# TensorE's order from the out-projection on: chosen by the scheduler, or as written

## Chip, cores, metric

The kernel runs on one core of a Trainium2 chip. The metric is the device time of one execution in microseconds (us), the median over several runs.

## What is computed

One decoder layer in float32 on 2048 tokens of width 1024. Attention and a gating unit share one input projection; their outputs, side by side, go through the out-projection, a residual and a layer norm, and then through a gated feed-forward net with 22 blocks of 128 hidden columns on either side (gate and up), again with residual and layer norm:

```python
mix = jnp.concatenate([attn, sgu], axis=-1) @ w_out[l] + b_out[l]
h = layer_norm(ALPHA * h + mix, ln_mix_g[l], ln_mix_b[l])
ffn = (jax.nn.silu(h @ w_gate[l]) * (h @ w_up[l])) @ w_down[l]
h = layer_norm(ALPHA * h + ffn, ln_ffn_g[l], ln_ffn_b[l])
```

The change touches these three matrix products (out, gate/up, down) and nothing ahead of them.

## The kernel before

**Units of seven products.** Each of the three matrix products is cut into units. A unit takes a 2 by 2 block of left tiles times a 2 by 2 block of right tiles with seven block products instead of eight (a Strassen-Winograd form). There are 76 units in a fixed order: 8 "o" (out-projection), 44 "g" (gate/up: half 0 of the tokens with 22 units, then half 1 with 22), 24 "d" (down-projection: three groups d0, d1, d2 of 8). A product is 4 matmul triples (3 in d0) of 512 columns; a triple is high times high, high times low, low times high part, since every float32 operand is split into a high and a low part.

**Order in a unit.** `CHAIN` is `a11→X, s1→Z, s2→X, s4→Z, s3→X, a12→Y, a22→X`: product → PSUM bank. X takes four products and Z two, one on top of the other. After each product a hook reads the bank, and the next product into that bank waits for that hook: s2 waits for the hook of a11, s4 for that of s1, s3 for that of s2, a22 for that of s3. In gate/up the hooks of a11, s1 and s2 are copies on ScalarE (L1114); those of s4, s3 and a12 are additions on VectorE (L1117), and that of s3 (`z<-X_g`) is the one that a22 waits for. The hook of a22 is L1132, and its result is stored by GpSimd (L1134). In "o" and "d" units all hooks are VectorE additions (L1030, L1032). "d2" also has a layer norm on VectorE (L133 to L167) and the stores of the output (L1178).

**Operands.** `Left.make(p)` makes the left operand of product p of the *next* unit right behind product p of this one: a sum on VectorE where needed (L888, L891, L894, L897), the high part on ScalarE (L864), the low part on VectorE (L865). Seven buffers hold a unit's left operands. `Right.make(p)` does the same for the right side (L929 on ScalarE, L930 on VectorE, differences L935 on VectorE), which changes only between stages: o to g half 0, half 0 to half 1, g to d0, d0 to d1, d1 to d2. There is one buffer for each of the seven right operands, so the new one is made after the last unit of the old side has used the old one. The right sides of g half 0 and of the d groups come ready-made (`pre`); that of half 1 also needs the L935 differences.

**Side work.** `combine` (L980 to L984) makes the d right sides in half 1, units 1 to 11, from loads L1152. `z_transpose` (L1074 on TensorE, 16 groups of 8) stands in units 1 to 8. `z_affine` runs in units 3 to 18 of half 0: a load of `za` on the SyncE queue (L1084), a multiplication and an addition on GpSimd over 128x1024 (L158, L159), and a store (L1086).

**What sets the order.** A scheduler with a timeline of its own orders each engine's instructions; every engine then takes its queue strictly in order and waits on semaphores. Before the change TensorE's queue is ordered in this way too. The line that issues all matmuls is L994, and the loop over the units stands at the end of `hybrid_block`.

Of the kernel before, what the change touches and what calls it, by code (L numbers as in the profile page):

```python
# [68 lines left out]
def hybrid_block(ctx, tc, x, pos, ln_col, ln_in_g, ln_in_b, wqkv, wsu, wsv, b_qkv, b_su, b_sv, sinks,  # L69
# [5 lines left out]
    def pool(stack, name, bufs, **kw):  # L75
        return stack.enter_context(tc.tile_pool(name=name, bufs=bufs, reuse_waits="tile", **kw))
# [43 lines left out]
    def bcast(row_ap, name, p=None, tag="cst"):  # L120
        t = (p or cst).tile([P, D], F32, tag=tag, name=name, **({"bufs": 1} if tag == "rq" else {}))
        SP.dma_start(t, row_ap.partition_broadcast(P))
        return t
# [851 lines left out]
    def combine(nm, load, k):  # L975

        t = raw8(f"tc_{nm}_{k}").rearrange("p (q t) -> p q t", q=4)
        for n, q in enumerate(("b11", "b12", "b22", "b21")):
            load(q, t[:, n:n + 1], slice(k, k + 1))
        V.tensor_tensor(t[:, 0], t[:, 1], t[:, 0], ALU.subtract)  # L980
        V.tensor_tensor(t[:, 1], t[:, 2], t[:, 1], ALU.subtract)
        V.tensor_tensor(t[:, 2], t[:, 2], t[:, 0], ALU.subtract)
        V.tensor_tensor(t[:, 3], t[:, 3], t[:, 2], ALU.subtract)
        PL.dma_start(tD[nm][:, :, k, :], t)  # L984

    def unit(name, nk, left, right, hooks, after=None):
        bank = {}
        for n, (p, x_, first) in enumerate(CHAIN):
            if first:
                bank[x_] = psf.tile([P, 512], F32, tag="f", name=f"{x_}_{name}")  # L990
            lt, rt = left.t[p], right.t[BOF[p]]
            for k in range(nk):
                for m, (a, b) in enumerate(((0, 0), (0, 1), (1, 0))):
                    PE.matmul(bank[x_], lt[:, a, k, :], rt[:, b, k, :],  # L994
                              start=(first and k == 0 and m == 0),
                              stop=(k == nk - 1 and m == 2), skip_group_check=True)
            hooks[p](bank[x_])
            if after:
                after(p)


    def load_m(j):
        t = raw8(f"rm{j}").rearrange("p (e a c) -> p e a c", e=2, a=2)
        for e in range(2):
            for a in range(2):
                SP.dma_start(t[:, e, a], mixd[2 * j + e][a].rearrange("p k t -> p (k t)"))
        v = t.rearrange("p e a (k t) -> p e a k t", k=4)
        return Left(f"o{j}", (v[:, 0, 0], v[:, 0, 1], v[:, 1, 0], v[:, 1, 1]), 4)
# [44 lines left out]
    def o_hooks(j):  # L1053
        ac = hacc.pop(j)

        def done(e):
            i = 2 * j + e
            mu, rs = moments(ac[e])
            nmr = small.tile([P, 1], F32, tag="nmr", name=f"nmr{i}")
            V.tensor_scalar(nmr, mu, rs, -1.0, ALU.mult, ALU.mult)  # L1060
            A.activation(ac[e], ac[e], AF.Identity, bias=nmr, scale=rs)
            PL.dma_start(zd[i], ac[e])
            zs[i] = ac[e]

        return block_hooks(ac, True, done)

    def z_transpose(i):
        z = zs.pop(i)
        for j in range(2):
            ps = psf.tile([P, 512], F32, tag="f", name=f"ph{i}_{j}")  # L1070
            tr = trp.tile([P, 4, P], F32, tag="tr", name=f"tr{i}_{j}")
            for k in range(4):
                kk = 4 * j + k
                PE.transpose(ps[:, k * P:(k + 1) * P], z[:, kk * P:(kk + 1) * P], ident)  # L1074
            for k in range(4):
                kk = 4 * j + k
                A.activation(tr[:, k], ps[:, k * P:(k + 1) * P], AF.Identity,
                             bias=mcol[:, 1, kk:kk + 1], scale=mcol[:, 0, kk:kk + 1])
            PL.dma_start(h2T[i // 4][:, 4 * j:4 * j + 4, (i % 4) * P:(i % 4 + 1) * P], tr)


    def z_affine(i):
        t = ot.tile([P, D], F32, tag="o", name=f"za{i}")
        SP.dma_start(t, zd[i])  # L1084
        affine(t, t, fg[0], fg[1])
        PL.dma_start(h2d[i], t)  # L1086
# [9 lines left out]
    def h_load(h):  # L1096
        def load(q, t, ks=slice(0, 4)):
            c, kk = {"b11": (0, 0), "b12": (1, 0), "b21": (0, 1), "b22": (1, 1)}[q]
            SP.dma_start(t, h2T[2 * h + c][:, 4 * kk + ks.start:4 * kk + ks.stop, :])
        return load  # L1100
# [45 lines left out]
    def d_load(g):  # L1146
        f0, n = GROUPS[g]
        nk = n // 2

        def load(q, t, ks=slice(0, nk)):  # L1150
            kk, c = {"b11": (0, 0), "b12": (0, 1), "b21": (1, 0), "b22": (1, 1)}[q]
            SP.dma_start(t, w_down[f0 + kk * nk + ks.start:f0 + kk * nk + ks.stop, :,  # L1152
                                   c * 512:(c + 1) * 512].rearrange("f p c -> p f c"))
        return load
# [31 lines left out]
    def load_left(u):  # L1186
        return {"o": lambda _, j: load_m(j), "g": load_w, "d": load_a}[u[0]](*u[1:])

    def load_right(u):
        return {"o": lambda _: o_right(), "g": h_right, "d": d_right}[u[0]](u[1])  # L1190

    def load_out(u):
        if u[0] == "o":
            load_h(u[2])
        elif u[0] == "d":
            load_acc(*u[1:])
# [6 lines left out]
    for n, pc in enumerate(pieces):  # L1203
        forms["g", 1, 1 + n] = [pc]

    lefts[0] = load_left(units[0])
    rights[0] = load_right(units[0])
    load_out(units[0])
# [4 lines left out]
    for n, u in enumerate(units):  # L1213
        last = n + 1 == len(units)
        new = not last and units[n + 1][:2] != u[:2]
        if new:
            rights[n + 1] = load_right(units[n + 1])
            rights[n + 1].fetch()
        elif not last:
            rights[n + 1] = rights[n]  # L1220

        def after(p):
            if not last:
                lefts[n + 1].make(p)
            if new:
                rights[n + 1].make(p)
            if u in forms and p in ("s2", "a12"):
                for nm, k in forms[u][p == "a12":][:1]:
                    combine(nm, h_load(0) if nm == "h0" else d_load(int(nm[1])), k)
            if 0 < n <= NT // 2 and p in ("s4", "a12"):  # L1230
                z_transpose(2 * (n - 1) + (p == "a12"))

        if u == ("g", 0, 1):
            oo.close()
            fb_ = pool(ctx, "fb_", 2)
            fg = [bcast(mix_g, "mg", fb_, "f"), bcast(mix_b, "mb", fb_, "f")]
        if u == ("d", 1, 0):
            fg = [bcast(ffn_g, "fg", fb_, "f"), bcast(ffn_b, "fb", fb_, "f")]
        if u[0] == "g" and u[1] == 0 and 3 <= u[2] < 3 + NT:
            z_affine(u[2] - 3)  # L1240
        if not last:
            load_out(units[n + 1])
        hooks = {"o": lambda _, j: o_hooks(j), "g": gu_hooks, "d": d_hooks}[u[0]](*u[1:])
        nk = GROUPS[u[1]][1] // 2 if u[0] == "d" else 4
        unit("_".join(str(x_) for x_ in u), nk, lefts.pop(n), rights.pop(n), hooks, after)
        if n + 2 < len(units):
            lefts[n + 2] = load_left(units[n + 2])


# [56 lines left out]
```

## Time and profile before

| | |
|---|---|
| median of 3 runs | 1995.65 us (1995.31, 1995.65, 2001.1) |
| the profiled execution | 1998.47 us, span on the core 1996.4 us, mean granted TensorE clock 0.984 |
| TensorE matmuls busy | 1917.0 us, 96% of the span, 9126 instructions |
| VectorE busy | 1456.3 us, 73% |
| ScalarE busy | 843.2 us, 42% |
| GpSimd busy | 437.5 us, 22% |

The share of a whole span hides the stages, so the rows below go by stage and then to single waits. In a timeline row, what stands in brackets is how long the engine was idle just before the row and whose instruction ended that; a row with "x12" is 12 instructions in a run. PE is TensorE's matmul, PEld its weight load, DVE VectorE, ACT ScalarE, POOL GpSimd, SPq the queue of SyncE, which issues loads.

### The profile page before, as it was taken

The numbers are of one execution on the slowest core, as the hardware profiler recorded it, in microseconds if no ns is written. First come the engines' busy times: TensorE is split into PE (matmuls) and PEld (weight loads), VectorE is DVE, ScalarE is ACT, GpSimd is POOL, SyncE is SP. The second block draws the span as 40 slices with busy tenths as digits, with TensorE's granted clock in tenths as the row PEclk, the third lists the DMA queues.
The fourth block names the chain that finished last, engine by engine and source line by source line (L and its number), as shares of the span: only waits on it lengthen the run. The fifth ranks groups of instructions, "written<-read, shape, count | busy, mean of one in ns | idle before, by whom it ended". The sixth has DMA issues, their size and how long they took to land.

```text
span 1996.4 us, 24982 instructions
## 1 busy us (share of the span) xinstructions
PE 1917.0 (96%) x9126; PEld 1581.7 (79%) x9126; DVE 1456.3 (73%) x2335; ACT 843.2 (42%) x1637; POOL 437.5 (22%) x431
## 2 busy tenths in 40 slices
PE   5699999999999999999999999999999999999997
PEld 4587878799787888888888887888888787887876
DVE  6769998676877876766765976655556869668997
ACT  4466667632364763333333533333334324224220
POOL 1246766311032223332320000000000000000212
PEclk8799999999999999999999999999999999999999
DMA  9044443796667963333342475631223668557532
GB/s 317 13 136 140 143 148 117 158 302 237 231 212 235 342 239 148 116 148 124 141 158 75 158 253 187 214 148 65 94 72 126 229 232 305 181 176 257 176 108 105
DMA packets 154810, 347.56 MB, mean 174 GB/s; under 512 B 11328, under 2 KB 74816, under 8 KB 151104
## 3 DMA queue, kind: packets, MB, share of 16 engines
q1 hardware_dynamic: 119488, 231.67, 34.3%
q0 software_dynamic: 35200, 114.31, 15.9%
q8 instruction: 71, 1.16, 0.2%
q14 instruction: 51, 0.42, 0.1%
HBM read 219.06 MB, written 126.88 MB: 173 GB/s over the span
## 4 chain that ended last, share of the span: by engine, by line
PE 77%; DVE 9%; DMA 6%; issue 3%; ACT 3%; POOL 2%; SPq 0%; POOLq 0%; DVEq 0%; ACTq 0%
PE X_g L994 22%; PE Z_g L994 11%; PE X_d L994 10%; PE Y_g L994 6%; PE Z_d L994 5%; PE pu L601 5%; PE X_o L994 4%; PE Y_d L994 3%; PE pq L330 2%; PE psv L562 2%; PE Z_o L994 2%; DMA tc_d<-in_w_down 1%; PE pkv L330 1%; PE Y_o L994 1%; DVE st L133 1%
## 5 line engine op out<-in xcount | busy, mean ns | idle before, releaser
L864 ACT ACTIVATE ws<-s 128x512 fp32r<-128x512 f32 x176 | 109.8, 626 | 202.2 <-DVE s L897 106.4
L865 DVE TENSOR_TENSOR ws<-s,ws 128x512 fp32r<-128x512 f32 x176 | 134.8, 768 | 60.4 <-ACT ws L864 59.8
L864 ACT ACTIVATE wa<-rw 128x512 fp32r<-128x512 f32 x132 | 82.1, 627 | 194.7 <-PE X_g L994 168.9
L1134 POOL DMA_DIRECT2D aD<-x x44 | 23.7, 540 | 599.5 <-DVE x L1132 586.9
L994 PE MATMUL Y_g<-b21t_h,wa 128*128 128x512 f32 x528 | 140.7, 396 | 0.1
L994 PE MATMUL Z_g<-t1t_h,ws 128*128 128x512 f32 x528 | 136.5, 395 | 0.0
L994 PE MATMUL X_g<-b11t_h,wa 128*128 128x512 f32 x528 | 131.8, 397 | 0.0
L994 PE MATMUL X_g<-t4t_h,wa 128*128 128x512 f32 x528 | 130.5, 395 | 0.8 <-DVE z L1117 0.7
L994 PE MATMUL X_g<-t2t_h,ws 128*128 128x512 f32 x528 | 130.6, 395 | 0.0
L864 ACT ACTIVATE ws_d<-s_d 128x512 fp32r<-128x512 f32 (+1 forms) x96 | 56.0, 594 | 175.1 <-PE X_d L994 70.2
L994 PE MATMUL Z_g<-b22t_h,ws 128*128 128x512 f32 x528 | 128.8, 392 | 0.0
L994 PE MATMUL X_g<-t3t_h,ws 128*128 128x512 f32 x528 | 127.3, 390 | 0.0
L994 PEld LDWEIGHTS X_g<-t4t_h,wa 128*128 128x128 f32 x528 | 98.9, 188 | 25.5 <-DVE z L1117 1.6
L994 PEld LDWEIGHTS Y_g<-b21t_h,wa 128*128 128x128 f32 x528 | 99.1, 188 | 24.3 <-ACT wa L864 0.5
L994 PEld LDWEIGHTS Z_g<-t1t_h,ws 128*128 128x128 f32 x528 | 99.1, 188 | 24.1
L994 PEld LDWEIGHTS X_g<-t2t_h,ws 128*128 128x128 f32 x528 | 99.1, 188 | 24.1
L994 PEld LDWEIGHTS X_g<-b11t_h,wa 128*128 128x128 f32 x528 | 99.1, 188 | 23.8
L994 PEld LDWEIGHTS Z_g<-b22t_h,ws 128*128 128x128 f32 x528 | 99.1, 188 | 22.9
L1132 DVE TENSOR_TENSOR x<-X_g,x 128x512 f32<-128x512 f32 x44 | 30.3, 689 | 118.5 <-PE X_g L994 118.4
L994 PEld LDWEIGHTS X_g<-t3t_h,ws 128*128 128x128 f32 x528 | 99.1, 188 | 21.0
L330 PE MATMUL pq<-wq,hT 128*128 128x512 f32 x384 | 96.7, 402 | 1.3 <-DVE at L486 1.2
L865 DVE TENSOR_TENSOR wa<-rw,wa 128x512 fp32r<-128x512 f32 x132 | 90.4, 687 | 10.3 <-ACT wa L864 9.5
(283 smaller groups left out, 4337.2 us busy)
## 6 DMA issues: line engine op xcount, KB each, us to landing
rw<-in_w_gate SPq DMA_DIRECT2D x44, 512.0 KB, 3.9
rw<-in_w_up SPq DMA_DIRECT2D x44, 512.0 KB, 4.8
aD<-x POOLq DMA_DIRECT2D x44, 512.0 KB, 3.0
hTd<-hT SPq DMA_DIRECT2D x16, 1024.0 KB, 7.2
hTg<-hTd POOLq DMA_DIRECT2D x8, 2048.0 KB, 9.5
accd<-da POOLq DMA_DIRECT2D x32, 512.0 KB, 3.8
ra<-aD SPq DMA_DIRECT2D x16, 1024.0 KB, 8.4
da<-accd SPq DMA_DIRECT2D x32, 512.0 KB, 3.5
```

The source lines that it names most:

```text
L133: V.bn_stats(st[:, j, :], src[:, j * 512:(j + 1) * 512])
L330: PE.matmul(ps[:, :c1_ - c0], t[:, a, k, :], wq[k][:, b, c0:c1_], start=(k == 0 and n == 0), stop=(k == KT - 1 and n == 2))
L562: PE.matmul(pv_, t[:, a, k, :], wsv_t[k][:, b, :], start=(k == 0 and n == 0), stop=(k == KT - 1 and n == 2))
L601: PE.matmul(pu[:, j, :], wsu_t[k][:, a, hs], t[:, b, k, :], start=(k == 0 and n == 0), stop=(k == KT - 1 and n == 2))
L864: A.activation(hi, src, AF.Copy)
L865: V.tensor_tensor(lo, src, f32b(hi), ALU.subtract)
L994: PE.matmul(bank[x_], lt[:, a, k, :], rt[:, b, k, :], start=(first and k == 0 and m == 0), stop=(k == nk - 1 and m == 2), skip_group_check ...
L1132: V.tensor_tensor(v["x1"], ps, v["x1"], ALU.mult)
L1134: PL.dma_start(aD[g][h][:, e, :], v["o"].rearrange("p a t -> p (a t)"))
```

## The change

Around the loop over the units a manual schedule is switched on for TensorE alone. TensorE's instructions from the first out-projection matmul to the last keep the order in which the code writes them: one product after the other, one unit after the other. The orders of the other engines are still chosen by the scheduler, now around that given TensorE order.

```diff
@@ end of hybrid_block @@
+    written = ExitStack()
+    written.enter_context(tc.manual_schedule(engines={mybir.EngineType.PE}))
     lefts[0] = load_left(units[0])
...
         if n + 2 < len(units):
             lefts[n + 2] = load_left(units[n + 2])
+    written.close()
```

In the names below, `X_g_0_10` is bank X of gate/up half 0, unit 10; `wa22_0_10` is its left operand for a22, `ws1` that of s1; `t4t_h0` is the right operand of a22, `b21t` that of a12, `b11t` that of a11. First TensorE in half 0, where unit 9 goes over into unit 10, before:

```order
L994 MATMUL X_g_0_10_8581<-b11t_h0_6958,wa11_0_10_8460 128x512 x12
L994 MATMUL Z_g_0_10_8599<-t1t_h0_6984,ws1_0_10_8480 128x512 x11
L994 MATMUL X_g_0_9_8445<-t4t_h0_7171,wa22_0_9_8434 128x512 x12
L994 MATMUL Z_g_0_10_8599<-t1t_h0_6984,ws1_0_10_8480 128x512
L994 MATMUL Y_g_0_10_8674<-b21t_h0_7115,wa12_0_10_8553 128x512
L994 MATMUL X_g_0_10_8581<-t2t_h0_7009,ws2_0_10_8498 128x512 x12
L994 MATMUL Y_g_0_10_8674<-b21t_h0_7115,wa12_0_10_8553 128x512 x11
L994 MATMUL Z_g_0_10_8599<-b22t_h0_7033,ws4_0_10_8516 128x512 x12
L994 MATMUL X_g_0_10_8581<-t3t_h0_7080,ws3_0_10_8535 128x512 x12
```

and after:

```order
L994 MATMUL X_g_0_9_8447<-t3t_h0_7082,ws3_0_9_8401 128x512 x12
L994 MATMUL Y_g_0_9_8540<-b21t_h0_7117,wa12_0_9_8419 128x512 x12
L994 MATMUL X_g_0_9_8447<-t4t_h0_7173,wa22_0_9_8436 128x512 x12
L994 MATMUL X_g_0_10_8583<-b11t_h0_6960,wa11_0_10_8462 128x512 x12
L994 MATMUL Z_g_0_10_8601<-t1t_h0_6986,ws1_0_10_8482 128x512 x12
L994 MATMUL X_g_0_10_8583<-t2t_h0_7011,ws2_0_10_8500 128x512 x12
L994 MATMUL Z_g_0_10_8601<-b22t_h0_7035,ws4_0_10_8518 128x512 x12
L994 MATMUL X_g_0_10_8583<-t3t_h0_7082,ws3_0_10_8537 128x512 x12
```

Between s3 of a unit (`t3t`) and its a22 (`t4t`) stood a11 and s1 of the next unit, 23 matmuls; now a12 of the same unit stands there, 12 matmuls, and no product is cut in pieces.

Next VectorE in the same unit after the change, from the last hook of unit 9 to the hook that a22 of unit 10 waits for:

```order
L1132 TENSOR_TENSOR x1_0_9_8460<-X_g_0_9_8447,x1_0_9_8460 128x512
L865 TENSOR_TENSOR wa22_0_10_8572<-rw0_10_8439,wa22_0_10_8572 128x512
L865 TENSOR_TENSOR wa11_0_11_8598<-rw0_11_8575,wa11_0_11_8598 128x512
L865 TENSOR_TENSOR ws1_0_11_8618<-s1_0_11_8616,ws1_0_11_8618 128x512
L888 TENSOR_TENSOR s1_0_12_8752<-rw0_12_8711 128x512
L865 TENSOR_TENSOR ws2_0_11_8636<-s2_0_11_8634,ws2_0_11_8636 128x512
L897 TENSOR_TENSOR s2_0_11_8634<-rw0_11_8575,s2_0_11_8634 128x512
L1117 TENSOR_TENSOR x1_0_10_8596<-Z_g_0_10_8601,x1_0_10_8596 128x512
L865 TENSOR_TENSOR ws4_0_11_8654<-s2_0_11_8634,ws4_0_11_8654 128x512
L891 TENSOR_TENSOR s2_0_12_8770<-s1_0_12_8752,rw0_12_8711 128x512
L1117 TENSOR_TENSOR z1_0_10_8614<-X_g_0_10_8583,z1_0_10_8614 128x512
```

Before, the same stretch had the addition from bank Y ahead of that from bank Z, and the split `wa22` stood ahead of L1132, not behind it.

Last TensorE where half 0 ends (unit 21) and half 1 begins, before:

```order
L994 MATMUL X_g_1_0_10244<-b11t_h1_10086,wa11_1_0_10083 128x512
L994 MATMUL X_g_0_21_10068<-t3t_h0_7080,ws3_0_21_10021 128x512 x12
L994 MATMUL X_g_1_0_10244<-b11t_h1_10086,wa11_1_0_10083 128x512 x11
L994 MATMUL Z_g_1_0_10262<-t1t_h1_10113,ws1_1_0_10108 128x512 x12
L994 MATMUL X_g_0_21_10068<-t4t_h0_7171,wa22_0_21_10056 128x512 x12
```

and after:

```order
L994 MATMUL X_g_0_21_10070<-t3t_h0_7082,ws3_0_21_10023 128x512 x12
L994 MATMUL Y_g_0_21_10196<-b21t_h0_7117,wa12_0_21_10041 128x512 x12
L994 MATMUL X_g_0_21_10070<-t4t_h0_7173,wa22_0_21_10058 128x512 x12
L994 MATMUL X_g_1_0_10246<-b11t_h1_10088,wa11_1_0_10085 128x512 x12
L994 MATMUL Z_g_1_0_10264<-t1t_h1_10115,ws1_1_0_10110 128x512 x12
```

Here too the two products of the next unit that stood between s3 and a22 of unit 21 have moved behind its a22.

## Rows read from the trace of the kernel before

**Rows 1.** Busy us (instructions) of each engine by stage, TensorE clock, DMA.

```profile
core 0: us, PE busy (x) PEld busy (x) DVE busy (x) ACT busy (x) POOL busy (x), PEclk, DMA share, GB/s
512.00:686.00 174.00, 168.47 (x769) 136.42 (x770) 137.20 (x244) 97.90 (x188) 40.34 (x59) 0.98 0.72 251
686.00:1113.00 427.00, 427.00 (x1852) 345.71 (x1851) 296.53 (x375) 169.58 (x300) 113.66 (x80) 1.00 0.40 146
1113.00:1540.00 427.00, 426.08 (x1833) 343.71 (x1832) 273.35 (x415) 161.30 (x276) 19.77 (x33) 1.00 0.42 147
1540.00:1986.00 446.00, 441.94 (x1895) 354.73 (x1893) 357.40 (x560) 131.71 (x208) 48.51 (x62) 1.00 0.57 198
```

**Rows 2.** TensorE timeline: start, length, operation, [idle before it, released by].

```profile
366.43 5.49 PE L562 MATMUL psv<-wsv_b,h 128*128 128x512 f32 x12 [3.63 <-DVE hl L459]
...
519.39 3.04 PE L994 MATMUL X_o<-t2t_o,ws_o 128*128 128x512 f32 x12 [1.22 <-DVE hb L1030]
...
640.59 5.31 PE L994 MATMUL X_o<-t4t_o,wa_o 128*128 128x512 f32 x12 [4.21 <-DVE hb L1032]
...
1241.62 3.06 PE L994 MATMUL X_g<-t4t_h,wa 128*128 128x512 f32 x12 [0.72 <-DVE z L1117]
...
1678.76 0.50 PE L994 MATMUL Y_d<-b21t_d,wa_d 128*128 128x512 f32 x1 [0.90 <-ACT b21t_d L929]
...
1983.11 3.04 PE L994 MATMUL X_d<-t4t_d,wa_d 128*128 128x512 f32 x12 [1.15 <-DVE da L1032]
```

**Rows 3.** Windows around the wait at 640 us; columns as in the first group.

```profile
630.00:640.60 10.60, 6.39 (x33) 4.98 (x31) 10.60 (x23) 5.81 (x12) 3.46 (x5) 0.91 0.75 260
640.60:646.00 5.40, 5.40 (x15) 4.29 (x16) 2.08 (x6) 1.26 (x2) 1.70 (x3) 0.54 0.98 249
```

**Rows 4.** Timeline of all engines, one gate/up unit of half 0.

```profile
941.55 2.98 PE L994 MATMUL X_g<-b11t_h,wa 128*128 128x512 f32 x12
...
943.18 0.68 DVE L1117 TENSOR_TENSOR z<-X_g,z 128x512 f32<-128x512 f32 x1
943.78 0.68 DVE L865 TENSOR_TENSOR wa<-rw,wa 128x512 fp32r<-128x512 f32 x1
...
945.27 0.69 DVE L865 TENSOR_TENSOR wa<-rw,wa 128x512 fp32r<-128x512 f32 x1 [0.21 <-ACT wa L864]
945.99 0.33 SPq L1091 DMA_DIRECT2D rw<-in_w_gate  x1
...
946.90 0.37 SPq L1084 DMA_DIRECT2D za<-zd  x1
946.92 2.96 PE L994 MATMUL X_g<-t4t_h,wa 128*128 128x512 f32 x12
...
949.72 0.40 PE L994 MATMUL Z_g<-t1t_h,ws 128*128 128x512 f32 x1
...
952.69 2.58 POOL L158 TENSOR_TENSOR za<-za,mg 128x1024 f32<-128x1024 f32 x1 [1.24 <-DMA za<-zd]
...
954.34 1.48 DVE L865 TENSOR_TENSOR ws<-s,ws 128x512 fp32r<-128x512 f32 x1 [1.33 <-ACT ws L864]
...
955.35 2.74 POOL L159 TENSOR_TENSOR za<-za,mb 128x1024 f32<-128x1024 f32 x1
...
955.85 2.78 DVE L897 TENSOR_TENSOR s<-rw,s 128x512 f32<-128x512 f32 x1
```

**Rows 5.** Timeline, VectorE and TensorE, where half 0 goes over into half 1.

```profile
1102.65 2.36 DVE L930 TENSOR_TENSOR b11t_h<-b_h,b11t_h 128x1024 fp32r<-128x1024 f32 x2 [0.74 <-ACT b11t_h L929]
1104.93 2.35 DVE L935 TENSOR_TENSOR b_h<-b_h,b_h 128x1024 f32<-128x1024 f32 x2
...
1120.49 0.68 DVE L1117 TENSOR_TENSOR z<-X_g,z 128x512 f32<-128x512 f32 x1
...
1122.62 2.96 PE L994 MATMUL X_g<-t4t_h,wa 128*128 128x512 f32 x12
```

**Rows 6.** VectorE's waits, 1130 to 1400 us: who, for whom: us, times, longest.

```profile
DVE tc_d L980 <- DMA tc_d<-in_w_down: 39.4, 8, 7.3
```

## The prediction

> **What bounds the kernel now.** I read the stages first. From the out-projection to the last matmul TensorE is busy 168.47 of 174, 427 of 427, 426.08 of 427 and 441.94 of 446 us [rows 1]: it stands still for 5.53 + 0 + 0.92 + 4.06 = 10.5 us in 1474, and nothing else bounds this part. Then I looked for where it stands still. The large waits are 1.22 us at 519, 4.21 at 640, 0.72 at 1241, 0.90 at 1678 and 1.15 at 1983 [rows 2]; the rest are pieces under 1 us. In all of gate/up, 44 of the 76 units, there is one. The reader is to see in [rows 2] that most waits end on VectorE or on a split of an operand: TensorE waits for hooks and operands, not for loads. One more price: behind the 4.21 us the 12 matmuls took 5.31 us, where 12 elsewhere start 2.80 us apart (946.92 to 949.72) [rows 2, 4], about 2.35 us more; the granted clock there was 0.54 [rows 3], near the lower of its two levels (1.2 of 2.4 GHz). So the most that any order can give back is 10.5 + 2.35 = 12.9 us.
>
> **What the change takes away.** Not one matmul goes; only their places move. In the order of before, a11 and s1 of the next unit lie between s3 and a22 of a unit, so that the hook of s3 has some 5.4 us (941.55, where s3 ends, to 946.92) [rows 4]. In the written order only a12 lies there: 2.80 us. Against that stands that a12 is always there. The wait of 4.21 us is an out-projection unit in which a22 follows directly on s3; this case disappears, with its 2.35 us. I first count the 12.9 us as given back in full, and then add every wait that the written order makes, those that come again among them.
>
> Durations for that: a VectorE instruction over 128x512 starts 0.60 us after the one before (943.18, 943.78) [rows 4], one over 128x1024 takes 2.28 / 2 = 1.14 (1102.65 to 1104.93) [rows 5]. A unit is 7 x 2.80 = 19.6 us, in d0, with 9 matmuls for 12, 14.7. I count from the start of a11 (t = 0), so s3 ends at 14.0 and a22 is due at 16.8, and I take VectorE's instructions in the order that it has after the change.
>
> **Gate/up, half 0, with GpSimd's affine (16 units).** Without side work the hook of s3 starts at 14.0 and ends at 14.7: 2.1 us early. But [rows 4] show what GpSimd does to VectorE. L158 runs from 952.69 to 955.27 and L159 from 955.35 to 958.09; the split L865 that starts at 954.34 takes 1.48 us for 0.69 and ends 0.55 after L158; L897 takes 2.78 and ends 0.54 after L159. A VectorE instruction that falls under L158 or L159 is held to its end. Where does that pair fall now? The load of za is issued behind the loads of the weights, and these wait for the split wa22 (945.27, then 945.99); L158 starts 952.69 - 946.90 = 5.8 us after the issue of za [rows 4]. After the change wa22 is made at t = 0.7 to 1.4, za is issued at 2.3, and L158 starts at 8.1; the store of the unit's result, issued at about 0.8, now goes ahead of these loads. Three transfers of 512 KB land in 952.69 - 945.99 = 6.7 us, so a fourth can add up to a third, 2.2; I take 8.1 to 9.6 as likely. With 8.1 the split of ws2 (due at 9.1) is held to 11.2 and L897 to 14.0, then four instructions, and the hook of s3 ends at 16.4: just in time. With 9.3 L897 is held to 12.4 and, if an addition from PSUM is held as well, the Z hook to 15.2; the hook of s3 ends at 17.0: 0.3 late. With 11 it is 18.1: 1.4 late. No row shows an L1117 under L158 or L159, so between 0 and 1.4 us a unit is open; I take 0.25, near the 8.1 to 9.6 that the rows give: 16 x 0.25 = **4.0 us** (0 to 22). Cover before: 5.4 us, so it was free.
>
> The Trainium skill, page "SBUF — State Buffer", section "Who interferes with whom", says that a VectorE instruction with two SBUF inputs contends with a GpSimd instruction that reads SBUF, and one with at most one SBUF input does not. L865 and L897 held, as above, agree with the first half; for the second no row here has the case. By it the term would be near 0 in place of 4.0, and the hook of s3 itself never held.
>
> **Half 0 to half 1.** The right side of half 1 is made while unit 21 runs. Up to the hook of s3 VectorE has, behind the first halves of b11t at t = 5.0: 5 splits L930 and 5 differences L935 of 1.14, and 4 instructions of 0.60: 5.0 + 11.4 + 2.4 = 18.8, end 19.5. Before, the same hook ran at 1120.49 and a22 started at 1122.62 without a wait [rows 5], covered by a11 and s1 of half 1. Now a22 is due at 16.8: 2.8 us late. Behind it stand three more L930 and one L935, three left splits and two hooks ahead of the second half of t2t, so s2 of the new unit waits about 2.0 us more, and its a22, behind b21t, t4t and two L935, about 1.7. Together **6.5 us** (3 to 11, with one drop of the clock).
>
> **The borders of the down-projection.** d0 to d1, by the same count: between the a11 hook of d0's last unit (t = 2.7) and its s3 hook VectorE has six L930, two left splits and four hooks; the s3 hook ends at 14.2 and a22 is due at 12.6: 1.65. Then eight more instructions, five of 1.14, lie ahead of the hook of a11 of d1 that s2 waits for: 2.8. Together 4.45, where before TensorE waited 0.90 at 1678 [rows 2]. d1 to d2 has the same instructions in units of 19.6 us rather than 14.7: 2.4. g to d0: 1.1. Together **7.9 us** (4 to 11).
>
> **The out-projection.** Its first unit waits for the X_o hook of a11 as before (1.22 at 519 [rows 2]); since s1 now runs unbroken and the hook does not come earlier, 1.9, and behind it 1.2 for the operands of a12 and a22, which are still being split. The first unit of gate/up waits 1.8 for t3t and b21t of its new right side. Together **4.9 us** (3 to 7). The other o units have 21.4 us with the transposes and no wait by count.
>
> **Half 1 with combine; d2; the end.** VectorE now waits up to 7.3 us for a load at L980 [rows 6], and its place in the queue moves: in units 6 to 10 L980 stands a few rows earlier, right behind the splits. Whoever is queued behind it (ws splits with a unit's time in hand, the Z hook, the s3 hook) is late by that wait; with the largest wait, 7.3 us from t = 2.5 on, and eleven instructions of 0.60 behind it the s3 hook ends at 17.1, 0.3 late; with the mean, 39.4 / 8 = 4.9 us, it ends at 14.7, in time: 0 (0 to 4). In d2 VectorE also carries the layer norms; over the whole stage it is busy 357.40 of 446 us [rows 1], so a hook can come late there too: 0 (0 to 4). The last hook of row block e1 now follows a12's layer norm at only 2.8 us: **0.5** (0 to 1).
>
> **The sum.** 4.0 + 6.5 + 7.9 + 4.9 + 0.5 = 23.8 us of waits made, less 12.9 taken away: **+11 us**. The profiled execution took 1998.47 us (span 1996.4, the rest outside it), 2.8 above the median of 1995.65; I put the difference on the median: 1995.65 + 11 = 2006.7, say **2007 us**.
>
> **Rivals.** *The waits are covered (faster).* VectorE's order is chosen anew around the written TensorE order, and if it and the loads bring the hooks at the four borders 2 to 3 us earlier than I count, the borders cost what they cost now. Then 12.9 - 4.9 (out-projection and first unit) = 8 us are gained: 1988. It decides at one point: the s3 hook of unit 21 must end by t = 16.8. Against it: 18.8 is a sum of VectorE work alone, without any wait. *About the same.* Half of the border waits and little of the affine: 23.8 - 7.2 - 3 = 13.6 against 12.9, near 1997. *PSUM additions are not held by GpSimd:* the affine term is 0, 2003. The Trainium skill's page "SBUF — State Buffer" says so (above). *Each unit of half 0 waits:* L158 at t = 11 or later, 1.4 x 16 = 22 for 4, and the three waits of 2 to 3 us at borders each drop the clock: behind a wait of 3.63 us 12 matmuls took 5.49 us [rows 2], no row shows what a wait of 2 to 3 us does. 2007 + 18 + 3 x 2.35 = 2032. That the change would not do what it says is excluded by the order of TensorE's instructions.
>
> **Chances.** Measurement can tell 0.3%, 6 us, from no change. My forecast (2004 to 2014) 0.42; PSUM additions not held, 2003: 0.15, a third of it inside 0.3%; each unit waits, 2018 and up: 0.16; about the same: 0.14; covered: 0.13. Slower by over 0.3%: 0.42 + 0.10 + 0.16 = 0.68, less 0.05 for the part of the forecast that lands under it: 0.63. Same: 0.24. Faster: 0.13. The range reaches down to the covered case at 1989 and up into the case where each unit waits, 2026; I leave out the ends of both.
>
> **What would show it.** Right: TensorE's waits in [rows 1] grow from 10.5 to some 24 us; the row at 640 is gone with its clock of 0.54; new waits before `X_g<-t4t_h` released by L1117, a short one in each of 16 units of half 0 and one of 2 to 3 us where half 1 begins; waits before `X_d<-t4t_d` and `X_d<-t2t_d` at the starts of d1 and d2. Wrong: no wait in half 0 (GpSimd's pair falls earlier, or PSUM additions pass), or gate/up with waits in half 1 as well, where I count none: then VectorE's loads of combine decide, and the slack of 2.1 us is not there.

## The result, and the profile after

The changed kernel takes 2023.56 us (median of 5 runs, 2020.46 to 2028.44); the kernel before, in 5 runs on the same chip, 1995.65 us. The ratio is 1.0137, 95% interval 1.0119 to 1.0156: slower by 27.9 us. The sign of the prediction holds, and the time lies inside its range; its size does not hold: it said 2007, 11 us slower, and the change cost two and a half times that. The profiled execution took 2024.12 us with a span of 2022.4, that is 26.0 over the span before.

The windows view of the kernel after, by the stages of [rows 1] (columns as there; with a fifth stretch, because the last matmul now ends at 2011.5):

```profile
512.00:686.00 174.00, 170.32 (x787) 138.03 (x788) 141.99 (x249) 100.40 (x191) 40.76 (x60) 1.00 0.74 254
686.00:1113.00 427.00, 413.67 (x1772) 329.73 (x1771) 290.71 (x358) 164.39 (x287) 110.05 (x78) 1.00 0.39 142
1113.00:1540.00 427.00, 421.30 (x1806) 339.63 (x1805) 275.72 (x408) 165.60 (x272) 19.77 (x33) 1.00 0.41 145
1540.00:1986.00 446.00, 438.72 (x1874) 352.00 (x1874) 359.36 (x550) 142.18 (x220) 42.35 (x58) 1.00 0.58 201
1986.00:2012.00 26.00, 25.53 (x110) 20.28 (x109) 18.66 (x30) 1.90 (x3) 4.82 (x5) 1.00 0.17 61
```

TensorE's idle time in the out-projection fell from 5.53 to 3.68 us. In gate/up it rose from 0 and 0.92 to 13.33 and 5.70, in the down-projection from 4.06 to 7.28: in these four stages 30.0 us for 10.5, where the prediction had some 24. Half 0 of gate/up, which had no wait at all, is now the worst stage. Who ends the waits, from the end of the first gate/up unit to the last matmul (waits view of the kernel after, TensorE; us in total, times, longest):

```profile
PE X_g L994 <- DVE z L1117: 17.0, 19, 2.7
PE X_d L994 <- DVE da L1032: 6.6, 7, 1.9
PE X_g L994 <- ACT x L1114: 0.9, 1, 0.9
...
```

Nearly all are hooks on VectorE; none is for a load or for an operand. 16 of the 19 in the first row are in the 16 units of half 0 that have GpSimd's affine. One of them in TensorE's timeline, from its a11 to the next:

```profile
748.36 2.96 PE L994 MATMUL X_g<-b11t_h,wa 128*128 128x512 f32 x12
...
762.24 2.98 PE L994 MATMUL Y_g<-b21t_h,wa 128*128 128x512 f32 x12
765.97 3.06 PE L994 MATMUL X_g<-t4t_h,wa 128*128 128x512 f32 x12 [0.76 <-DVE z L1117]
768.87 2.96 PE L994 MATMUL X_g<-b11t_h,wa 128*128 128x512 f32 x12
```

From a11 to a11 it is 768.87 - 748.36 = 20.51 us, where an unhindered unit takes 19.49. A wait costs more than its bracket: behind a running product the next one starts 2.80 us after it, but a12's modelled end, from which the bracket counts, is 2.98 after its start; and the first product after a wait holds up the next by 2.90 instead of 2.80. 0.76 + 0.18 + 0.10 = 1.04.

Where the 26.0 us of span come from, with 19.49 us for an unhindered unit and 14.63 in d0:

| stretch of the kernel after | forecast | measured | from |
|---|---|---|---|
| start of the out-projection | 0 | +0.6 | 511.89 before, 512.53 after |
| out-projection and first gate/up unit, net | -3.0 | -2.6 | a11 of the second gate/up unit: 710.31 before, 708.39 after, less the 0.6 |
| half 0, 16 units with GpSimd's affine | +4.0 | **+16.4** | 16 x (20.52 - 19.49) |
| half 0 to half 1 | +6.5 | +6.2 | units of 23.90 and 21.24 us |
| half 1 with combine | 0 | +2.0 | the waiting one at 1236.83 |
| three borders of the down-projection | +7.9 | **+11.4** | 437.45 us from 1571.12 to 2008.57, less 426.1 |
| end | +0.5 | +0.5 | span less last matmul's end |
| waits of before that go, behind the first gate/up unit | -5.0 | -8.6 | 1272.80 us from 710.31 to 1983.11, less 1264.2 |
| sum | 10.9 | 25.9 | span: 26.0 |

### The profile page after: what moved, and what is told of

Its sections match the earlier page's. It is cut to its first block, busy times and chain, and to the rows that moved or that the text cites. A ratio compares the mean times of both kernels' runs of the same rounds, so it can differ in the third digit from the quotient of the medians.

```text
span 2022.4 us, 25214 instructions
## 1 busy us (share of the span) xinstructions
PE 1922.7 (95%) x9126; PEld 1580.8 (78%) x9126; DVE 1477.5 (73%) x2335; ACT 856.5 (42%) x1637; POOL 433.7 (21%) x431
## 3 DMA queue, kind: packets, MB, share of 16 engines
q0 software_dynamic: 35200, 114.31, 16.8%
## 4 chain that ended last, share of the span: by engine, by line
PE 68%; DVE 17%; ACT 5%; DMA 4%; issue 3%; POOL 1%; SPq 0%; POOLq 0%; ACTq 0%; DVEq 0%
PE X_g L994 19%; PE X_d L994 10%; PE Z_g L994 8%; PE Z_d L994 5%; PE pu L601 5%; PE X_o L994 4%; PE Y_g L994 3%; PE Y_d L994 3%; DVE ws L865 2%; PE pq L330 2%; DVE s L897 2%; PE psv L562 2%; PE Z_o L994 2%; DMA tc_d<-in_w_down 1%; DMA tD_d<-tc_d 1%
## 5 line engine op out<-in xcount | busy, mean ns | idle before, releaser
L865 DVE TENSOR_TENSOR ws<-s,ws 128x512 fp32r<-128x512 f32 x176 | 145.0, 825 | 127.0 <-ACT ws L864 126.1
L864 ACT ACTIVATE ws<-s 128x512 fp32r<-128x512 f32 x176 | 110.1, 627 | 157.2 <-DVE s L897 97.2
L994 PE MATMUL Y_g<-b21t_h,wa 128*128 128x512 f32 x528 | 131.2, 397 | 0.3 <-DVE b21t_h L930 0.3
L994 PE MATMUL Z_g<-t1t_h,ws 128*128 128x512 f32 x528 | 130.3, 395 | 0.0
L864 ACT ACTIVATE ws_d<-s_d 128x512 fp32r<-128x512 f32 (+1 forms) x96 | 56.8, 596 | 158.6 <-PE X_d L994 62.6
L864 ACT ACTIVATE wa<-rw 128x512 fp32r<-128x512 f32 x132 | 82.6, 628 | 91.9 <-PE Y_g L994 60.8
L1114 ACT ACTIVATE x<-X_g 128x512 f32<-128x512 f32 x88 | 52.7, 599 | 153.2 <-PE X_g L994 151.1
```

The costliest lines, as they stand in the source:

```text
L864: A.activation(hi, src, AF.Copy)
L865: V.tensor_tensor(lo, src, f32b(hi), ALU.subtract)
L994: PE.matmul(bank[x_], lt[:, a, k, :], rt[:, b, k, :], start=(first and k == 0 and m == 0), stop=(k == nk - 1 and m == 2), skip_group_check ...
L1114: A.activation(v[nm], ps, AF.Copy)
```

## Experiments

The largest item is half 0. Theory A: GpSimd's pair L158, L159 holds VectorE's instructions with two SBUF operands just ahead of the hook of s3; under the written order only a12 covers that hook, so each of the 16 units waits. The main rivals: VectorE's queue under the written order is too long by itself, whatever GpSimd does; or the pair costs time under any order of TensorE. If A holds, a second question follows: is it the pair's work that costs, or only where in the unit it falls? Each ratio below is to runs of the kernel before that were taken beside it (medians 1996.64 to 1997.2 us).

**The pair left out of the changed kernel.**

```diff
@@ z_affine @@
-        affine(t, t, fg[0], fg[1])
```

> The written order, with GpSimd's multiplication and addition in z_affine (L158, L159) left out; the load of za and its store stay. Order of TensorE and of VectorE as in the changed kernel. Theory A (GpSimd's pair holds VectorE's ws2 split and L897, so the s3 hook is late and a22 waits): the 16 waits of 0.5 to 1.4 us before X_g<-t4t_h in half 0 go, a unit there takes 19.5 us instead of 20.5, in all 16.4 us less: about 2007. Rival B (the hook is late because a12 alone, 2.80 us, is too little cover for VectorE's queue, or because the za load and the store crowd the weights' loads): the waits stay, 2020 to 2024.

Measured: 2008.83 us, ratio to before 1.0057 (1.0042 to 1.0072): 14.7 us less than the changed kernel. The 16 waits are gone, and those at the borders stay. The windows view of this kernel, 720 to 1100 us (columns as in [rows 1]), has TensorE busy throughout:

```profile
720.00:1100.00 380.00, 380.00 (x1639) 307.55 (x1638) 213.39 (x316) 139.51 (x235) 19.70 (x37) 1.00 0.36 132
```

**The same edit in the kernel before.**

> The kernel before with L158 and L159 left out (za is loaded and stored unchanged, so the mask is not applied), TensorE in the order of the kernel before. A control for the affine term. Theory A (GpSimd's pair delays VectorE's hook of s3, and under the order of before a11 and s1 of the next unit lie between s3 and a22 and cover that delay): no change of the time, 1996 +- 3, ratio 0.9985 to 1.0015, and the units of half 0 stay at 19.49 us. Rival (the pair costs time under any order, through the queue or the SBUF): 1996 less about 12 us, 1984, as much as leaving the pair out took from the changed kernel.

Measured: 1997.1 us, ratio 1.0001 (0.9991 to 1.0010). Under the scheduler's order the pair costs nothing that can be measured. So its price comes with the new TensorE order, and the rival of a price under any order falls. The run does not show that the shorter cover alone makes that price. Over the 16 units of the kernel before, the hook of s3 ends 2.3 us after s3 in 14 of them and 3.1 us at most (943.18 + 0.68 against 941.55 [rows 4]), so that 2.80 us would have covered nearly all of them; in the changed kernel it ends 3.4 to 4.3 us after s3. The pair itself has moved towards the hook: L158 starts 7.4 to 8.6 us ahead of the end of s3 before, and 3.6 to 5.2 us ahead of it after the change. A cover of 5.4 us would have covered those too. So by these numbers the wait needs both, the cover of 2.80 us and the later place of the pair.

**The pair's work on VectorE instead.** If the length of VectorE's queue were the cause, two more instructions of 1.22 us in each unit would make it worse.

```diff
@@ z_affine @@
-        affine(t, t, fg[0], fg[1])
+        affine(t, t, fg[0], fg[1], V)
```

> The written order, with the multiplication and addition of z_affine on VectorE instead of GpSimd: 2 x 1.14 us more of VectorE's own work in each of 16 units, and nobody holds it. Theory A: the hold costs VectorE 0.8 + 2.1 us in the one stretch where it has 2.0 us of slack; 2.3 us of work that the scheduler can place early in the unit do not: waits in half 0 mostly gone, 2007 to 2012. Rival C': 2.3 us more in VectorE's queue are as bad as the hold: 2018 or more.

Measured: 2006.61 us, ratio 1.0053 (1.0038 to 1.0068). No wait in these units, though VectorE has two instructions more in each. They stand in the same part of the unit as GpSimd's pair (L158 at t = 951.27 - 942.51 = 8.8 from the start of a11) and take 1.23 and 1.22 us. The rival of the long queue falls.

**The load of `za` one unit earlier.**

```diff
@@ z_affine, and the loop over the units @@
+    def z_load(i):
...
+        if u[0] == "g" and u[1] == 0 and 2 <= u[2] < 2 + NT:
+            z_load(u[2] - 2)
```

> The written order, all work kept; only the load of za is issued one unit earlier, so that L158 can start right behind the store of the unit's result, at about t = 1.5 us after the start of a11 instead of 8.9. Theory A: L158 and L159 then lie at 1.5 to 7 us and hold splits that have a unit's time in hand (wa11, ws1); the s3 hook ends at 14.7 and the 16 waits go: about 2007, as with the affine left out. Rival C (VectorE loses the same time wherever it is held, since its queue is in order): the waits stay, above 2018.

Measured: 2022.86 us, ratio 1.0127 (1.0112 to 1.0142), the waits much as in the changed kernel. It doesn't answer the second question, because the pair did not move. In GpSimd's timeline of this kernel it still stands right behind a load of `za`, at t = 940.67 - 931.68 = 9.0 of its unit:

```profile
940.67 2.40 POOL L158 TENSOR_TENSOR za<-za,mg 128x1024 f32<-128x1024 f32 x1 [7.21 <-DMA za<-zd]
```

The scheduler, still free on GpSimd, had drawn the pair forward to the newest load.

**The same, with GpSimd's order written out as well in half 0.**

```diff
@@ the loop over the units @@
+        if u == ("g", 0, 2):
+            pool_written = ExitStack()
+            pool_written.enter_context(tc.manual_schedule(engines={mybir.EngineType.Pool}))
+        if u == ("g", 0, 20):
+            pool_written.close()
```

> All work kept, TensorE and VectorE in the order of the changed kernel. The load of za is written one unit earlier, and in half 0 GpSimd's order is written too, so that L158 and L159 cannot follow the newest load: they should run behind the store of the last unit's result, at about t = 1.5 to 7 us after the start of a11, where they can hold only splits with a unit's time in hand. Theory A (what counts is where the pair falls: under the ws2 split and L897 it makes the s3 hook late): the waits in half 0 go, 2006 to 2010, as with the affine left out (2008.8). Rival C (the 4 us that VectorE loses are lost wherever the pair falls): waits stay, 2020 or more.

Measured: 2005.63 us, ratio 1.0047 (1.0032 to 1.0062), with all of the work in it. A unit of this kernel, all engines:

```profile
936.22 2.98 PE L994 MATMUL Y_g<-b21t_h,wa 128*128 128x512 f32 x12
936.42 0.69 DVE L1122 TENSOR_TENSOR z<-X_g,z 128x512 f32<-128x512 f32 x1 [0.58 <-PE X_g L994]
...
939.03 2.96 PE L994 MATMUL X_g<-t4t_h,wa 128*128 128x512 f32 x12
...
941.83 2.96 PE L994 MATMUL X_g<-b11t_h,wa 128*128 128x512 f32 x12
...
943.64 2.41 POOL L158 TENSOR_TENSOR za<-za,mg 128x1024 f32<-128x1024 f32 x1
...
946.13 2.80 POOL L159 TENSOR_TENSOR za<-za,mb 128x1024 f32<-128x1024 f32 x1
```

The pair now runs from t = 1.8 to 7.1, and the hook of s3 (L1122 here) starts as soon as s3 is done. No VectorE instruction of this unit takes over 0.70 us: the pair meets none that it holds, not even the splits with time in hand that were expected to be held. So the cost hangs on where in the unit GpSimd works, not on its work. Half 0 in the windows view, 720 to 1100 us (columns as in [rows 1]), of the changed kernel:

```profile
720.00:1100.00 380.00, 367.81 (x1568) 292.97 (x1567) 253.20 (x301) 129.81 (x224) 103.12 (x68) 1.00 0.35 129
```

The same stretch of the kernel in which VectorE does the pair's work:

```profile
720.00:1100.00 380.00, 380.00 (x1639) 307.48 (x1638) 240.50 (x348) 137.48 (x234) 19.71 (x37) 1.00 0.36 131
```

And of this kernel, with GpSimd's order written out:

```profile
720.00:1100.00 380.00, 380.00 (x1639) 307.45 (x1638) 212.89 (x315) 139.62 (x234) 104.26 (x69) 1.00 0.36 130
```

TensorE is busy throughout in the last two. In the changed kernel VectorE is busy 253.20 us with 301 instructions, in the last one 212.89 us with 315: the difference is time in which it was held.

**Written order in one part only.** Three kernels switch it on from the out-projection to the end of the first gate/up unit; in units 1 to 20 of half 0; in the 24 units of the down-projection. The first as a diff:

```diff
@@ the loop over the units @@
+        if n == NT // 2:
+            written.close()
-    written.close()
```

> The written order only up to the end of the first gate/up unit; from there TensorE is ordered by the scheduler as in the kernel before. Theory A: the 4.21 us wait at 640 us and its slow 12 matmuls are gone (-6.6), the new waits of the out-projection and of the first gate/up unit stay (+4), the rest is as in the kernel before: 1993, 2.6 us below it. Rival D (the waits only move to the place where the order is handed back): 1996 or more.

> TensorE's order as written only for gate/up half 0, units 1 to 20; everything ahead and behind is ordered by the scheduler. Theory A: 16 x 1.0 us against the kernel before, nothing else: 2012 to 2014. Rival E (the waits in half 0 are an outcome of the orders ahead, or are paid back later): under 2006.

> TensorE's order as written only from the first down-projection unit on. By the prediction the borders cost 7.9 us less what they cost before (some 4): about 2000 to 2001; by the trace of the changed kernel, whose d units stand 15 us over their undisturbed length where those of before stand some 4 over it: 2005 to 2008.

Measured, in this order: 1992.88 us, ratio 0.9981 (0.9971 to 0.9990), 4.0 us less; 2014.26 us, ratio 1.0091 (1.0076 to 1.0106), 17.1 us more; 2008.59 us, ratio 1.0064 (1.0048 to 1.0081), 11.4 us more. The first lands on its forecast, the second just above its own, the third above both of its estimates. The three add up to 24.5 us, where the whole change costs 27.9; the borders of half 1 and its combine are in none of them. The third is not a clean measure of its part: at its start TensorE waits 3.67 us for a hook at 1575, where the old order hands over to the new, and the 9 products behind that wait take 3.79 us for 2.34, together some 5 of its 11.4 us; the changed kernel has only waits of 0.32 and 0.39 there. The first kernel is the only one that beats the kernel before.

**A wider cover under the written order.** a22 of a unit is written behind a11 and s1 of the next, so that the hook of s3 has three products, not one.

```diff
@@ unit @@
+        for p, x_, first in CHAIN[:-1]:
+            product(p, x_, first)
+            if p == "s1" and held:
+                held()
+        return lambda: product(*CHAIN[-1])
```

> A written order all through, with another place for one product: a22 of a unit is written behind a11 and s1 of the next unit, as the scheduler had it in the steady state. Between s3 and a22 then lie a12, a11 and s1: 8.4 us instead of 2.80. Theory A: the s3 hook is never late for a22 (largest lateness so far 2.7 us), so the 16 waits, the 2.7 us at the half border and those before X_d<-t4t_d go, and the 4.21 us case of the out-projection cannot come back; what is left are waits of s2 at borders: 1987 to 1995. Rival B' (the order of the products does not matter, only that they are not cut): 2015 or more.

Measured: 2017.02 us, ratio 1.0097 (1.0082 to 1.0112); a miss: 1987 to 1995 was expected, and the time falls into the range of rival B'. In half 0 the waits are gone, a unit takes 946.01 - 926.52 = 19.49 us, as expected. But that cannot be put down to the cover, because the pair has moved as well:

```profile
948.98 2.39 POOL L158 TENSOR_TENSOR za<-za,mg 128x1024 f32<-128x1024 f32 x1 [8.98 <-DMA za<-zd]
```

L158 starts at t = 948.98 - 946.01 = 3.0 of its unit, L159 at 10.2, and the hook of s3 ends 0.9 to 1.3 us after s3 in these units, which 2.80 us would have covered too. So half 0 of this kernel decides neither between A and B' nor between cover and place. What was not foreseen are long waits elsewhere (TensorE's timeline of this kernel, three places):

```profile
655.36 4.63 PE L995 MATMUL Z_o<-b22t_o,ws_o 128*128 128x512 f32 x12 [6.60 <-DVE hb L1037]
...
1553.55 4.42 PE L995 MATMUL Z_g<-b22t_h,ws 128*128 128x512 f32 x12 [7.82 <-ACT z L1121]
...
1577.10 3.32 PE L995 MATMUL X_d<-t3t_d,ws_d 128*128 128x512 f32 x7 [2.40 <-DVE da L1037]
```

and what VectorE did ahead of the first, ScalarE ahead of the second:

```profile
646.99 0.69 DVE L980 TENSOR_TENSOR tc_h<-tc_h 128x512 f32<-128x512 f32 x1 [4.53 <-DMA tc_h<-h2T]
...
1552.90 0.60 ACT L1121 ACTIVATE z<-Z_g 128x512 f32<-128x512 f32 x1 [4.66 <-DMA aD<-x]
```

Ahead of the first wait the scheduler had put an instruction that needs a load in front of the hooks, and the load came late; ahead of the second the hook itself, a copy on ScalarE, stood, by the profile, until the store of a result (`aD<-x`) was through. TensorE, in its fixed order, had nothing else to take. The third was not traced further. A wider cover does not heal waits where another engine's queue stops for a transfer; what it does for the waits that repeat in each unit this kernel does not show.

## Where the prediction failed, and what of it held

**The affine term is the step that failed: 4.0 us forecast, 16.4 measured.** It makes up 12.4 of the 15 us of span by which the sum fell short. The mechanism was named, its size was not: the step that failed is the choice between the two cases, made with a split of ws2 due at t = 9.1, which gave 0.25 us a unit; the split comes at 9.75, under L158, and a unit is 1.03 us longer. VectorE, GpSimd and TensorE in one unit of the kernel after (a11 of the unit starts at 932.89):

```profile
941.49 0.60 ACT L1114 ACTIVATE x<-X_g 128x512 f32<-128x512 f32 x1 [1.68 <-PE X_g L994]
941.75 2.40 POOL L158 TENSOR_TENSOR za<-za,mg 128x1024 f32<-128x1024 f32 x1 [7.07 <-DMA za<-zd]
941.98 0.62 ACT L864 ACTIVATE ws<-s 128x512 fp32r<-128x512 f32 x1
942.64 2.06 DVE L865 TENSOR_TENSOR ws<-s,ws 128x512 fp32r<-128x512 f32 x1 [1.38 <-ACT ws L864]
...
944.22 2.74 POOL L159 TENSOR_TENSOR za<-za,mb 128x1024 f32<-128x1024 f32 x1
944.73 2.79 DVE L897 TENSOR_TENSOR s<-rw,s 128x512 f32<-128x512 f32 x1
...
946.77 2.97 PE L994 MATMUL Y_g<-b21t_h,wa 128*128 128x512 f32 x12
...
947.44 0.68 DVE L1117 TENSOR_TENSOR x<-Z_g,x 128x512 f32<-128x512 f32 x1
...
948.29 0.69 DVE L865 TENSOR_TENSOR ws<-s,ws 128x512 fp32r<-128x512 f32 x1 [0.18 <-ACT ws L864]
...
949.63 0.68 DVE L1117 TENSOR_TENSOR z<-X_g,z 128x512 f32<-128x512 f32 x1
...
950.37 0.97 PE L994 MATMUL X_g<-t4t_h,wa 128*128 128x512 f32 x3 [0.62 <-DVE z L1117]
```

The load lands where the prediction put it: L158 at t = 8.86 here, and at 8.7 to 9.6 in 14 of the 16 units, inside 8.1 to 9.6; in the other two it starts at 9.9 and 10.2. The forecast then had two cases: at 8.1 both the split of ws2 and L897 are held, at 9.3 the split is already through, since it was due at 9.1. In the trace it starts at 9.75. The count had left out that ScalarE first does the copy L1114 (941.49) and only then the high part L864 (941.98) that the split needs. The kernel before has it too: its split at 954.34 [rows 4] starts 1.35 us after s2 ends (952.99), where the count took 0.7. So L158 catches the split up to t = 9.7, and the first case was the one for the whole range. At its own t that case gives 16.4 + (8.86 - 8.1) = 17.2 for the end of the hook, 0.4 late; the measured lateness is 0.80 (a22 due at 946.77 + 2.80, started at 950.37). Of the rest, 0.25 is the split of ws4, which waits for ScalarE behind L897 (0.18) and starts 0.85 us after the addition instead of 0.60, so that the hook ends at t = 17.4; and a22 is due at 16.7, not 16.8. And each of the 16 units waits, by 0.51 to 1.38 us, wherever in 8.7 to 10.2 the pair starts. To take a value near zero between two cases, for something that repeats in a rhythm, was the second error: here the pair cleared the hook in no unit.

**PSUM additions are not held.** The prediction left this open and gave it a rival of its own at 2003 us. Later in half 0 an addition that reads PSUM falls wholly into L159 (timeline of the kernel after):

```profile
984.18 2.78 DVE L897 TENSOR_TENSOR s<-rw,s 128x512 f32<-128x512 f32 x1
...
986.49 2.74 POOL L159 TENSOR_TENSOR za<-za,mb 128x1024 f32<-128x1024 f32 x1
986.89 0.68 DVE L1117 TENSOR_TENSOR x<-Z_g,x 128x512 f32<-128x512 f32 x1
...
987.75 2.03 DVE L865 TENSOR_TENSOR ws<-s,ws 128x512 fp32r<-128x512 f32 x1 [0.18 <-ACT ws L864]
```

It takes 0.68 us, as ever, and the split behind it, with two SBUF operands, is held to 0.55 us after the end of L159. This is one of the two late units (a11 at 973.70, L158 at t = 10.2): the split of ws2 is through, the split of ws4 is held in its place, and a22 waits 0.61 us all the same. So the premise of that rival was right, and its time was wrong: the hooks pass, but they stand in the queue behind splits that are held. The Trainium skill, page "SBUF — State Buffer", section "Who interferes with whom", says that a VectorE instruction with at most one SBUF input, outside the modes that use two ports, does not contend with GpSimd; this row, 0.68 us, agrees. That the affine term would then be near 0, as the prediction put it, does not follow: the held splits and L897 are enough.

**Half 0 to half 1: right in the sum (6.5 forecast, 6.2 measured), in part by luck.** TensorE's timeline of the kernel after:

```profile
1134.24 4.46 PE L994 MATMUL X_g<-t4t_h,wa 128*128 128x512 f32 x12 [2.74 <-DVE z L1117]
...
1145.21 3.07 PE L994 MATMUL X_g<-t2t_h,ws 128*128 128x512 f32 x12 [0.91 <-ACT x L1114]
...
1156.88 3.06 PE L994 MATMUL X_g<-t4t_h,wa 128*128 128x512 f32 x12 [0.30 <-DVE z L1117]
```

The three places are those that were named; the hook of s3 was counted 2.8 late and the wait is 2.74. The other two were counted at 2.0 and 1.7 and are 0.91 and 0.30; in their stead the products behind the first wait ran 1.5 us long, which the 6.5 did not contain and which made up for them.

**The borders of the down-projection: mis-sized, 7.9 for 11.4.** g to d0 came as counted (0.32 + 0.39, with the restarts 1.2). At d0 to d1 (first two rows) and d1 to d2 (the others):

```profile
1689.36 3.39 PE L994 MATMUL X_d<-t4t_d,wa_d 128*128 128x512 f32 x9 [1.90 <-DVE da L1032]
...
1699.84 3.05 PE L994 MATMUL X_d<-t2t_d,ws_d 128*128 128x512 f32 x12 [1.01 <-DVE da L1032]
...
1858.18 3.03 PE L994 MATMUL X_d<-t2t_d,ws_d 128*128 128x512 f32 x12 [1.49 <-DVE da L1032]
...
1865.06 2.98 PE L994 MATMUL X_d<-t3t_d,ws_d 128*128 128x512 f32 x12 [0.98 <-DVE da L1032]
```

At d0 to d1 the two waits, 1.90 and 1.01, were counted 1.65 and 2.8; the units are 5.4 us long for 4.45, because the 9 + 12 products from 1689.36 on ran slow and a third wait, 0.26 us, comes behind. At d1 to d2 it is 4.5 for 2.4. There VectorE also waited for loads with hooks queued behind (VectorE's timeline of the kernel after):

```profile
1861.67 0.69 DVE L888 TENSOR_TENSOR s_d<-ra 128x512 f32<-128x512 f32 x1 [0.76 <-DMA ra<-aD]
...
1867.24 0.69 DVE L888 TENSOR_TENSOR s_d<-ra 128x512 f32<-128x512 f32 x1 [1.13 <-DMA ra<-aD]
```

The count had instructions only, and no load that arrives late.

**Half 1: 0 (0 to 4) forecast, 2.0 measured.** The case that the prediction described, once:

```profile
1234.28 0.69 DVE L980 TENSOR_TENSOR tc_d<-tc_d 128x512 f32<-128x512 f32 x1 [3.27 <-DMA tc_d<-in_w_down]
...
1236.09 0.68 DVE L1117 TENSOR_TENSOR z<-X_g,z 128x512 f32<-128x512 f32 x1
...
1236.83 3.07 PE L994 MATMUL X_g<-t4t_h,wa 128*128 128x512 f32 x12 [1.74 <-DVE z L1117]
```

It put L980 early in the unit, right behind the splits (t = 2.5); here it stood late (t = 1234.28 - 1218.23 = 16.05), two instructions ahead of the hook, and 3.27 us were enough where the forecast had found 7.3 to cost 0.3. A wait in half 1 was one of the prediction's own signs of being wrong.

**The out-projection and the end: right in the sum.** The wait of 4.21 us at 640 with its slow products [rows 2, 3] is gone, -2.6 us net for -3.0. The parts differ: the wait of s2 in the first unit was counted 1.9 and is 0.76, and one of 0.77 us at 661.25 was not counted. **What the change takes away further on** was set too low: 5.0 us for 8.6. The count took only the idle time of [rows 1]; by the same rule as above, each wait costs a little more than its bracket, and where the old order cut a product in pieces it may have lost some more; this remainder of 3.6 us was not traced to single places.

Of the rivals, "covered" fell at the point that it named: the hook of unit 21 was 2.7 us late. "Each unit of half 0 waits" is what happened, below its price (0.76 us of idle and 1.03 us of length a unit, not 1.4) and with L158 at t = 8.7 to 10.2, not at 11. That the measured time lies inside the range is owed to this rival, up to which the range was drawn.

## What to carry to other kernels

A fixed order on one engine only, with the others still scheduled freely, turns a late hook on them into a stall where the work between is too short: write down, for each product that reads an accumulator's hook, how many microseconds of other products lie between, and place slow work of neighbouring engines (GpSimd's above all) outside the stretch in which those hooks and the splits ahead of them run. Moving that work 7 us ahead, in a unit of 19.5, was worth 18 us here, no less than leaving it out. Even so the written order stayed 0.5% above the kernel before (2005.63 us), and the waits that were left in that kernel stand at the borders, in the out-projection and once in half 1 (0.58 us); only the stretch up to the first gate/up unit gained by the order (1992.88 us). Where something repeats in a rhythm, decide the case from the phase and multiply; don't take a small average between two cases.

## What the runs showed of the hardware that was not expected

What follows on a wait of 2 to 3 us differs from trace to trace. After the wait of 2.74 us for the hook of unit 21 the 12 products took 4.46 us in the changed kernel. In the windows view of that kernel the granted clock of that stretch is 0.64 as a mean, so a good part of it ran at the lower of the two levels, 1.2 of 2.4 GHz:

```profile
1134.20:1138.50 4.30, 4.26 (x12) 3.42 (x13) 4.30 (x5) 0.75 (x2) 0.00 (x0) 0.64 0.02 4
```

After the same wait of 2.74 us the 12 took 4.60 with the load of `za` a unit earlier, but 3.07, 3.07 and 3.06 us with the pair left out, moved, or on VectorE. TensorE's timeline of the kernel with the pair left out:

```profile
1118.05 3.07 PE L994 MATMUL X_g<-t4t_h,wa 128*128 128x512 f32 x12 [2.74 <-DVE z L1116]
...
1129.05 4.62 PE L994 MATMUL X_g<-t2t_h,ws 128*128 128x512 f32 x12 [2.33 <-ACT x L1113]
```

There the shorter wait was followed by the slow products (mean granted clock 0.63 from 1129.0 to 1133.6), and the longer one was not (1.00). After 1.90 us at the end of d0 the 9 products took 3.39 us in the changed kernel and 2.35 with the pair left out. The prediction took 2.35 us for a drop, from the wait of 4.21 us [rows 2]; the drops seen after 1.9 to 2.7 us cost 1.0 to 1.6, and came in some of the traces only. What decides it was not settled.
